# Carrying an expert's rows back to the tokens behind the next expert's second gate and up products

## The chip, the cores and the metric

The kernel runs on one core of a Trainium2 chip (trn2). The metric is the device time of one execution in microseconds (us). The core has a matrix engine (TensorE, called PE in the profile, with its weight loads as PEld), VectorE (DVE), ScalarE (ACT), GpSimd (POOL) and SyncE (SP). In this kernel SP issues the loads of the weights.

## The reference

A model of four layers on 256 tokens of 1024 channels: retention, forgetting attention, then a conformer convolution with a dense feed-forward layer, and a short gated convolution with a mixture of eight experts. The change lies in the mixture of experts, which takes the second half of the time:

```python
logits = (x @ w_router).astype(jnp.float32)
top_val, top_idx = lax.top_k(logits, 2)
wts = jax.nn.softmax(top_val, axis=-1)
gates = jnp.sum(one_hot(top_idx, 8) * wts[..., None], axis=-2)
out = jnp.zeros_like(x)
for e in range(8):
    h = silu(x @ w_gate[e]) * (x @ w_up[e])      # 1024 -> 3584
    out = out + gates[..., e:e + 1] * (h @ w_down[e])   # 3584 -> 1024
```

A layer norm of alpha * x + out follows and is the output. All of it is in float32.

## The kernel before, in words

**Weights.** All weights are streamed from memory once, in units of 1 MB ([128, 2048] in float32). `Stream` (lines 66 to 161) loads them ahead into a ring of raw tiles, ten of them in the expert phase; SP issues a load as soon as a tile is free. Before its use each unit is split exactly into a high part (`wH`, a cast on ScalarE, line 122) and a low part (`wL`, a subtraction on VectorE, line 123). There are three buffers for each part, so a unit can be split only when the unit three before it has been used. Every product is then three matmuls (`mm3`, lines 229 to 233): high by high, high by low, low by high. In the expert phase a unit is split in one piece.

**Experts.** The tokens of each expert are gathered into 128 slots beforehand, transposed and split (`gather_steps`, two experts at a time, in the steps n = 2 to 6 of the experts 1, 3 and 5). For each expert e there are seven steps n, each for 512 of the 3584 hidden columns. The loop of lines 1493 to 1518 writes one step as follows:

- `up(e, n)` (line 1371): the gate product (two units, 24 matmuls of 512 columns), its SiLU on ScalarE into `mh`, the up product (two units, 24 matmuls), and VectorE's multiplication of the two (line 1378).
- `down(*prev)` (line 1390): the down product of the step before (two units, 24 matmuls) into the expert's two accumulator banks `y[e]`. The first unit and the second unit each go through both halves of the output columns.
- `turn(h)` (line 1381): four transposes of the new `h` and the split of the result into `mhH` and `mhL`.

So the last down product of expert e - 1 stands in step 0 of expert e. Behind it, in step 0, come for each half `nh` of the 1024 columns:

- `y_split(e - 1, nh)` (line 1426): a cast on ScalarE and a subtraction on VectorE, from the accumulator bank into the tile of tag `hL` (one buffer). In the trace these are `hL<-acc` of lines 358 and 361.
- `slots_back(e - 1, nh)` (line 1430): per token tile one PSUM bank and two matmuls of 512 columns with the one-hot rows `ohT`, of the high and of the low part (lines 1437 and 1438). This is what carries the slots' rows back to the tokens.
- `add_back(e - 1, nh)` (line 1442): per token tile one VectorE instruction (line 1446) that multiplies by the router's gate and adds to the running sum `self.o`, which the trace calls `x`.

**PSUM.** Two pools of four banks each: `mm` (line 215) for gate and up products, transposes and carry-backs, and `acc` (line 218) for the accumulators `y[e]`, two banks for each expert.

**The order of the work.** The program is written in the order above, and a scheduler puts instructions on each engine's queue by that order as a priority: an instruction that by its model cannot start yet may be passed by a later one that can. Each engine then works through its queue strictly in that order and waits at the first instruction whose inputs or buffer are not there. A bank or buffer is handed to the next user when its last reader is through. `self.soon` (line 211) raises the priority of what is written inside it. The last expert's end (`down_last`, line 1403) has a carry-back of its own, which the change doesn't touch. A second pass over slots 128 to 255 stands behind a branch (line 1558).

Of the kernel before, what the change touches and what calls it, by code (L numbers as in the profile page):

```python
# [65 lines left out]
class Stream:  # L66
    """Weights in the order of their use: 1 MB loads run ahead as far as the rings of raw tiles
    allow, then each is split exactly into two parts that fp32r passes carry."""

    def __init__(self, K, split_bufs, pieces=2):  # L70
        self.K, self.SB, self.pieces = K, split_bufs, pieces
        self.units, self.raws, self.parts = [], {}, {}
        self.rings = []
        self.i = self.nl = self.ns = 0
        self.native = None
        self.side = {}
        self.after = 0      # units whose split stays behind what has been traced so far

    def beside(self, fn):
        """fn issues loads of its own in front of the next unit's."""  # L80
        self.side.setdefault(len(self.units), []).append(fn)

    def ring(self, pool, tag, bufs, upto=1 << 30):
        """Buffers for the raw units before unit upto."""
        self.rings.insert(0, [pool, tag, bufs, 0, upto])
# [50 lines left out]
    def ahead(self, n, behind=True):  # L136
        """Splits the next n units, behind what has been traced so far."""
        self.after = max(0, self.i + n - self.ns) if behind else 0
        self._split(self.i + n)

    def get(self, key, hold=0):
        """The next unit; hold: units got before that are still to be used."""
        k, _, split = self.units[self.i]
        assert k == key, (k, key)
        if self.native is not None:
            self.native[3] -= 1
            self.native = None
        self._split(self.i + 1)
        ahead = 0
        j = self.i + 1  # L150
        while j < len(self.units) and ahead < self.SB - 1 - hold:
            ahead += self.units[j][2]
            j += 1
        self._split(j)
        self._load()
        r = self.parts.pop(self.i)
        self.i += 1
        if not split:
            self.native = r[1]
            return r[0]  # L160
        return r
# [31 lines left out]
class Kern:  # L193
# [9 lines left out]
    def table(self, func, after):  # L203
        """Has ACT load func's table off the critical path, once `after` is there."""
        self.nc.scalar.activation(self.t(self.sp, [P, 1], "tab", bufs=2), after, func)

    def ld(self, dst, src):
        """A load that keeps its place among those of the weights."""
        self.tc.keep_in_program_order(self.nc.sync.dma_start(out=dst, in_=src))

    def soon(self, n=400):
        """What is traced inside goes ahead of work traced up to n instructions before."""
        return self.tc.high_priority(n)
# [21 lines left out]
    def behind(self, ins, prev):  # L235
        """ins goes after prev on their engine."""
        self.tc.add_manual_dep(ins.ins, prev.ins.name,
                               mybir.DependencyInfo(mybir.DependencyClass.NoSync, mybir.DependencyReason.DATA),
                               reason="order")

# [1 line left out]
    def proj_tok(self, key, after=None, begun=False):  # L242
        """[t, 512] per token tile, from two units of four k blocks; begun: by first_tok."""
        if begun:
            ps = self.fps
            self.tok_tile(self.fw, ps, 0, 1)
        else:
            ps = [self.mm() for _ in range(2)]
        for kh in range(begun, 2):
            self.tok_half(key, ps, kh)  # L250
            if after is not None:
                after()
        return ps

    def first_tok(self, key):
        """The first token tile's part of the first unit of a phase."""
        self.fps = [self.mm() for _ in range(2)]
        self.fw = self.st.get(key, 2)
        self.behind(self.tok_tile(self.fw, self.fps, 0, 0), self.pair_end)

    def proj_wst(self, key, hH, hL):
        """[n, t] for two blocks of 128 n, from one unit of eight k blocks."""
# [9 lines left out]
    def first_half(self, key):  # L272
        """The first token tile's part of a phase's first product, which needs nothing of the second tile."""
# [14 lines left out]
    def proj_two(self, key, key2, begun, between):  # L288
        """Two products as of proj_wst; between takes the first, returns the second. begun: by first_half."""
# [20 lines left out]
    def out_k2(self, key, acc, oH, oL, ks, first, last):  # L310
        """acc[tt][nh] += o[k block].T @ w rows, one unit of two k blocks; oH(k, tt) an AP."""
# [8 lines left out]
    def out_k4(self, key, acc, oH, oL, ks, nh, first, last):  # L320
        """The same for one half of n, one unit of four k blocks."""
# [7 lines left out]
    def out_last(self, key, acc, oH, oL, parts):  # L329
        """The last two units of a product, a token tile at a time; parts: (k blocks, nh, first, last) of each."""  # L330
# [32 lines left out]
    def rpow(self, src, n, eps, scale=1.0, tag="rstd"):  # L363
        """(src * scale + eps) ** -0.5 for a [128, n] AP."""
# [7 lines left out]
    def ln_stats(self, parts, eps):  # L372
        """mean and rstd ([128, 1] each) over the free axis of a list of [128, 512] APs."""
# [11 lines left out]
    def new_h(self, f=True, parts=True):  # L385
        """Channels by tokens, [128, 8, 256]: f32 and the two parts of it."""
# [4 lines left out]
    def turned(self, x, tt, nh):  # L391
        """x.T of one token tile and half of the channels: [128, 4, 128] in a bank."""
# [8 lines left out]
    def plain(self, x, tt):  # L401
        """Token tile tt of x into hT or hH and hL."""
# [9 lines left out]
    def affine(self, x, tt, A, B, f, H, L, func=AF.Identity):  # L412
        """func(A*x.T + B) of token tile tt, and its parts; A, B: [128, 8]."""
# [56 lines left out]
    def vectors(self):  # L470
        """The vectors along partitions."""
# [14 lines left out]
    def mod_start(self, parts):  # L486
        """Bias of four chunks of 512 columns, one per 32 partitions, and the sums' bank."""
# [20 lines left out]
    def shift_scale(self, m, i):  # L508
        """m: chunks shift lo, shift hi, scale lo, scale hi -> A = g*(1+scale), B = shift, [128, 8]."""
# [13 lines left out]
    def gate_row(self, m, i):  # L523
        """m: chunks gate0 lo, hi, gate1 lo, hi -> row i spread over the partitions, [128, 1024]."""
# [9 lines left out]
    def residual(self, acc, gate, tt):  # L534
        """x + gate * acc of token tile tt, and rsqrt of its mean square."""
# [216 lines left out]
    def fox(self):  # L752
# [3 lines left out]
        with self.tc.tile_pool(name="fox", bufs=1) as fp:  # L756
# [11 lines left out]
            def decay(ps):  # L768
                """log forget gates, [t, 16] per token tile."""
# [24 lines left out]
            def running(lf):  # L794
                """Their running sums."""
# [14 lines left out]
            def qk(key, g, is_q, begun=False):  # L810
                """Normed heads with the decay's columns: [t, head, 64 | 2] per token tile."""
# [32 lines left out]
            def stage_t(d):  # L844
                """Transposed q and k of one head, with the gains."""
# [35 lines left out]
            def stage_v(d0, d1):  # L881
                """o.T of two heads into oT[:, pair, :]."""
# [87 lines left out]
    def rows(self, g, b):  # L970
        """Vectors along the free axis, spread over the partitions."""
# [5 lines left out]
    def deepnorm(self, acc, gb, first, f=False, parts=True):  # L977
        """x = LN(alpha*x + acc)*g + b and its transposed parts; first() follows those of the first token tile."""
# [26 lines left out]
    def conv_rows(self):  # L1005
        """Tap rows by tap mod 4, the upper half of the channels 32 partitions further on, and the
        first 256 channels' as they are from partition 64 on."""
# [11 lines left out]
    def conv_weights(self):  # L1019
        """Taps as [tap mod 4 and channel, group of 32 channels, tap block], and by channel, [128, 2, 31]."""  # L1020
# [14 lines left out]
    def conformer(self):  # L1035
        nc = self.nc
        hH, hL = self.hH, self.hL
        with self.tc.tile_pool(name="conf", bufs=1) as cp:
# [71 lines left out]
            def taps_apart(k, js):  # L1110
                """A block of channels, tap by tap."""
# [118 lines left out]
    def route(self, tt):  # L1230
        """Router of one token tile: which two experts."""
# [27 lines left out]
    def slots(self, tt):  # L1259
        """The slots of one token tile in the first two experts."""  # L1260
# [15 lines left out]
    def counts(self):  # L1276
        """Tokens of each expert."""
# [15 lines left out]
    def route_weights(self, pool):  # L1293
        """Softmax over the two chosen logits, zero elsewhere; the largest count as an integer."""
# [23 lines left out]
    def gather_steps(self, es, base, oh=None, bank=None):  # L1318
        """Slots base..base+127 of the tokens of two experts: transposed parts per expert, and
        the one-hot rows that carry slots back to tokens; five steps, the last yields them."""  # L1320
# [34 lines left out]
    def experts(self, st, base):  # L1355
        """All experts over their slots base..base+127; adds their gated rows to self.o."""
# [46 lines left out]
        def down_last(e, HL):  # L1403
            """The last rows of the last expert, half of the columns at a time."""
# [25 lines left out]
        def slots_back(e, nh, yHL):  # L1430
            """The slots' rows at their tokens, of half of the columns."""
# [18 lines left out]
        def dense_gates():  # L1450
            """The first gates of the first expert, for all tokens: needs no routing."""
# [12 lines left out]
        def dense_gather(h, HLs):  # L1464
            """The rows of the first expert's slots."""
# [27 lines left out]
        for e, n in [(e, n) for e in range(N_EXP) for n in range(7)]:  # L1493
# [9 lines left out]
            else:  # L1503
                h = up(e, n, None, lambda: None)
            down(*prev)
            with self.soon(60 if st.i >= len(st.units) - 2 else 0):
                prev = (e, n, turn(h))
            if e and n == 0:
                yHL = y_parts()
                for nh in range(2):  # L1510
                    y_split(e - 1, nh, yHL)
                    add_back(e - 1, nh, slots_back(e - 1, nh, yHL))
# [8 lines left out]
    def rest(self):  # L1521
        """Gates, alpha * x and the largest count."""
# [117 lines left out]
    def startup(self):  # L1640
        """The first block's input, half of the channels at a time, and with each half the products that it allows."""
# [143 lines left out]
```

## Time and profile before

| what | us |
|---|---|
| median of 3 runs | 1878.39 |
| lowest and highest run | 1877.34, 1884.4 |
| span of the profiled execution | 1873.6 |
| PE busy | 1809.3 |
| VectorE busy | 1415.0 |
| ScalarE busy | 1064.7 |

The span runs from the first to the last instruction of one profiled execution. No time of that execution from outside is listed, so its span stands beside the median of the runs: 1878.39 - 1873.6 = 4.8 us lie around it. A matmul of 512 columns shows as some 0.4 us long though the next one starts 0.23 us after it, since matmuls are pipelined; so the starts are what counts. Idle time in brackets at the end of a row is the engine's idle time just before the instruction, and what ended it.

### The profile page before, as it was taken

To read this page: it belongs to the slowest core of one execution; us is meant where nothing else is said; L and a number is where in the kernel's file an instruction comes from. 1 tells how busy PE (TensorE), PEld (TensorE's weight loads), DVE (VectorE), ACT (ScalarE), POOL (GpSimd) and SP (SyncE) were. 2 spreads that over 40 slices of the span, in tenths; PEclk is the share of its full clock that TensorE was granted. 3 is DMA by queue.
4 is the path that set the end of the run, shared out by engine and by line. 5 is a ranking of instruction groups with operands and counts; after the bars stand their busy time and mean duration, and the time that the engine had idled before them with its cause. 6 is when DMAs were issued, how large, how long until landed. Compare 5 with 4: busy or idle time off the path is not lost. (4 is left out here: it accounts for less than half of the span.)

```text
span 1873.6 us, 24361 instructions
## 1 busy us (share of the span) xinstructions
PE 1809.3 (97%) x9741; PEld 1486.5 (79%) x9741; DVE 1415.0 (76%) x1469; ACT 1064.7 (57%) x1036; POOL 65.7 (4%) x112
## 2 busy tenths in 40 slices
PE   6999999999999999999999999999999999999996
PEld 3867778789689998987878878878778788788785
DVE  3656666667775557679888888888888888888887
ACT  3333445654443433347767767767767677677673
POOL 1000003001100001000000000000000000000000
PEclk9999999999999999999999999999999999999998
DMA  9677646237356557548999989999999999999991
GB/s 356 233 274 243 224 141 202 77 113 252 114 180 190 188 184 243 195 147 316 346 359 340 362 297 363 369 340 337 349 319 365 360 342 355 316 349 366 332 365 68
DMA packets 252615, 509.34 MB, mean 272 GB/s; under 512 B 12347, under 2 KB 68782, under 8 KB 251470
## 3 DMA queue, kind: packets, MB, share of 16 engines
q1 hardware_dynamic: 249550, 500.64, 76.3%
q0 software_dynamic: 2592, 6.97, 1.2%
q8 instruction: 78, 1.28, 0.3%
q14 instruction: 43, 0.35, 0.1%
q10 hardware_dynamic: 352, 0.10, 0.0%
HBM read 504.28 MB, written 1.05 MB: 270 GB/s over the span
## 5 line engine op out<-in xcount | busy, mean ns | idle before, releaser
L123 DVE TENSOR_TENSOR wL<-raw,wH 128x2048 fp32r<-128x2048 f32 (+2 forms) x582 | 1033.9, 1801 | 258.7 <-ACT wH L122 257.6
L122 ACT CAST wH<-raw 128x2048 fp32r<-128x2048 f32 (+2 forms) x582 | 870.4, 1517 | 466.4 <-PE mm L233 144.3
L231 PE MATMUL mm<-hH,wH 128*128 128x256 f32 x816 | 232.2, 285 | 0.0
L232 PE MATMUL mm<-hL,wH 128*128 128x256 f32 x816 | 231.6, 284 | 0.0
L233 PE MATMUL mm<-hH,wL 128*128 128x256 f32 x816 | 231.2, 283 | 0.3 <-DVE wL L123 0.3
L231 PE MATMUL mm<-wH,hH 128*128 128x512 f32 (+1 forms) x512 | 200.4, 393 | 4.9 <-ACT wH L122 2.6
L232 PE MATMUL mm<-wL,hH 128*128 128x512 f32 (+1 forms) x512 | 199.4, 389 | 1.0 <-DVE wL L123 1.0
L232 PE MATMUL acc<-wL,mhH 128*128 128x512 f32 x448 | 178.5, 399 | 0.0
L233 PE MATMUL acc<-wH,mhL 128*128 128x512 f32 x448 | 176.6, 394 | 0.0
L231 PE MATMUL acc<-wH,mhH 128*128 128x512 f32 x448 | 166.8, 395 | 0.0
L231 PEld LDWEIGHTS mm<-hH,wH 128*128 128x128 f32 x816 | 156.5, 192 | 5.4 <-ACT wH L122 2.5
L233 PEld LDWEIGHTS mm<-hH,wL 128*128 128x128 f32 x816 | 156.5, 192 | 1.4 <-DVE wL L123 1.3
L232 PEld LDWEIGHTS mm<-hL,wH 128*128 128x128 f32 x816 | 156.6, 192 | 0.6 <-issue 0.2
L231 PE MATMUL mm<-wH,hT 128*128 128x512 f32 x336 | 133.1, 396 | 3.5 <-DVE x L1446 3.5
L231 PE MATMUL mm<-wH,xg 128*128 128x512 f32 x328 | 131.0, 399 | 3.5 <-DVE x L1446 3.5
L232 PE MATMUL mm<-wL,hT 128*128 128x512 f32 x336 | 132.7, 395 | 0.4 <-DVE wL L123 0.4
L233 PE MATMUL mm<-wH,hT 128*128 128x512 f32 x336 | 132.0, 393 | 0.0
L232 PE MATMUL mm<-wL,xg 128*128 128x512 f32 x328 | 130.8, 399 | 0.1
L233 PE MATMUL mm<-wH,xg 128*128 128x512 f32 x328 | 130.0, 396 | 0.0
L231 PEld LDWEIGHTS mm<-wH,hH 128*128 128x128 f32 x512 | 98.2, 192 | 30.9 <-ACT wH L122 3.6
L232 PEld LDWEIGHTS mm<-wL,hH 128*128 128x128 f32 x512 | 98.3, 192 | 21.7 <-DVE wL L123 3.5
L233 PE MATMUL mm<-wH,hL 128*128 128x512 f32 (+1 forms) x288 | 110.9, 385 | 0.7 <-DVE hL L361 0.7
(376 smaller groups left out, 2422.6 us busy)
## 6 DMA issues: line engine op xcount, KB each, us to landing
raw<-in_moe_w_gate_dram SPq DMA_DIRECT2D x112, 1024.0 KB
raw<-in_moe_w_up_dram SPq DMA_DIRECT2D x112, 1024.0 KB
raw<-in_moe_w_down_dram SPq DMA_DIRECT2D x111, 1024.0 KB
raw<-in_ret_w_in_dram SPq DMA_DIRECT2D x24, 1024.0 KB
raw<-in_mod_w_dram SPq DMA_DIRECT2D x32, 512.0 KB
raw<-in_fox_w_in_dram SPq DMA_DIRECT2D x16, 1024.0 KB
raw<-in_sc_w_in_dram SPq DMA_DIRECT2D x12, 1024.0 KB
raw<-in_ffn_w_gate_dram SPq DMA_DIRECT2D x11, 1024.0 KB
```

Of the source, the lines that this page charges most:

```text
L122: ops = (K.nc.scalar.copy(H[:, s], raw[:, s]), K.nc.vector.tensor_tensor(L[:, s], raw[:, s], H[:, s], op=ALU.subtract))
L123: K.nc.vector.tensor_tensor(L[:, s], raw[:, s], H[:, s], op=ALU.subtract))
L231: self.mm_first = mmul(ps, sH, mH, start=first, stop=False)
L232: mmul(ps, sH, mL, start=False, stop=False)
L233: self.mm_last = mmul(ps, sL, mH, start=False, stop=last)
```

## The change

The carry-back and the add are taken out of the loop over halves behind the split, in step 0, and stand in step 1 of the same expert, behind its gate and up products and ahead of the down product of step 0. The split stays where it was. The last expert's end stays as it was. The rest of the diff empties comments and docstrings, line by line, so that the lines above this place keep their numbers.

```diff
                 prev = (0, 0, turned[0])
             else:
                 h = up(e, n, None, lambda: None)
+            if e and n == 1:
+                for nh in range(2):
+                    add_back(e - 1, nh, slots_back(e - 1, nh, yHL))
             down(*prev)
             with self.soon(60 if st.i >= len(st.units) - 2 else 0):
                 prev = (e, n, turn(h))
...
                 yHL = y_parts()
                 for nh in range(2):
                     y_split(e - 1, nh, yHL)
-                    add_back(e - 1, nh, slots_back(e - 1, nh, yHL))
             if e % 2 and e < N_EXP - 1 and n >= 2:
```

## Rows read from the trace of the kernel before

**Rows 1.** The page's span and its totals by engine: busy us, share of the span, instructions.

```profile
span 1873.6 us, 24361 instructions
PE 1809.3 (97%) x9741; PEld 1486.5 (79%) x9741; DVE 1415.0 (76%) x1469; ACT 1064.7 (57%) x1036; POOL 65.7 (4%) x112
```

**Rows 2.** Windows: the seven steps with a carry-back, with their sum; columns in Rows 3.

```profile
971.70:992.61 20.91, 19.71 (x85) 15.22 (x84) 18.62 (x15) 13.41 (x10) 0.00 (x0) 1.00 0.91 315
1098.57:1123.29 24.72, 22.34 (x86) 17.24 (x84) 19.29 (x15) 13.30 (x10) 0.00 (x0) 0.86 0.77 268
1225.19:1247.45 22.26, 19.66 (x86) 15.16 (x84) 19.36 (x15) 13.38 (x10) 0.00 (x0) 1.00 0.91 315
1355.62:1379.20 23.58, 20.98 (x85) 16.31 (x84) 19.22 (x15) 13.39 (x10) 0.00 (x0) 0.93 0.84 285
1480.79:1502.81 22.02, 19.42 (x85) 15.17 (x84) 19.22 (x15) 13.39 (x10) 0.00 (x0) 1.00 0.90 323
1609.04:1632.83 23.79, 21.19 (x85) 16.30 (x84) 19.43 (x15) 13.39 (x10) 0.00 (x0) 0.93 0.83 285
1735.96:1759.45 23.49, 20.89 (x86) 16.30 (x85) 19.32 (x15) 13.39 (x10) 0.00 (x0) 0.93 0.86 301
sum 160.77, PE 144.19 PEld 111.70 DVE 134.46 ACT 93.67 POOL 0.00; mean PE 20.60 PEld 15.96 DVE 19.21 ACT 13.38 POOL 0.00
```

**Rows 3.** Windows: the seven plain steps behind those, first and sum, under the columns.

```profile
core 0: us, PE busy (x) PEld busy (x) DVE busy (x) ACT busy (x) POOL busy (x), PEclk, DMA share, GB/s
992.61:1009.57 16.96, 16.96 (x78) 13.88 (x76) 14.87 (x9) 12.43 (x8) 0.00 (x0) 1.00 1.02 372
...
sum 119.27, PE 119.27 PEld 97.13 DVE 100.96 ACT 87.08 POOL 0.00; mean PE 17.04 PEld 13.88 DVE 14.42 ACT 12.44 POOL 0.00
```

**Rows 4.** Waits of PE from 860 to 1830 us: total us, times, longest.

```profile
PE mm L231 <- DVE x L1446: 8.9, 5, 1.8
PE mm L1437 <- ACT hL L358: 5.1, 6, 0.9
```

**Rows 5.** Timeline of PE at the change to expert 5: start us, us, instruction.

```profile
1486.83 0.63 PE L1437 MATMUL mm<-hL,ohT 128*128 128x512 f32 x2
...
1488.78 0.73 PE L1437 MATMUL mm<-hL,ohT 128*128 128x512 f32 x2 [0.83 <-ACT hL L358]
1491.29 0.50 PE L231 MATMUL mm<-wH,hH 128*128 128x512 f32 x1 [1.77 <-DVE x L1446]
```

**Rows 6.** Timeline of DVE, the same change and the two steps behind it.

```profile
1488.28 2.29 DVE L123 TENSOR_TENSOR wL<-raw,wH 128x2048 fp32r<-128x2048 f32 x1 [0.51 <-ACT wH L122]
1490.49 1.40 DVE L1446 SCALAR_TENSOR_TENSOR x<-mm,rgate,x 128x512 f32<-128x512 f32 x2
1491.81 0.68 DVE L361 TENSOR_TENSOR hL<-acc,hL 128x512 fp32r<-128x512 f32 x1
...
1499.99 4.54 DVE L123 TENSOR_TENSOR wL<-raw,wH 128x2048 fp32r<-128x2048 f32 x2 [0.92 <-ACT wH L122]
1504.45 0.68 DVE L1378 TENSOR_TENSOR mh<-mh,mm 128x512 f32<-128x512 f32 x1
...
1519.97 0.69 DVE L1378 TENSOR_TENSOR mh<-mh,mm 128x512 f32<-128x512 f32 x1 [0.73 <-PE mm L233]
```

**Rows 7.** Timeline of ACT at the same change.

```profile
1485.86 0.58 ACT L358 CAST hL<-acc 128x512 fp32r<-128x512 f32 x1 [0.57 <-PE acc L233]
1486.34 1.91 ACT L122 CAST wH<-raw 128x2048 fp32r<-128x2048 f32 x1
```

**Rows 8.** Windows: the start, the expert phase, a stretch without carry-back; columns as Rows 3.

```profile
10.00:50.00 40.00, 32.77 (x214) 19.83 (x207) 19.21 (x36) 14.76 (x23) 4.61 (x9) 0.91 1.05 385
860.00:1820.00 960.00, 942.82 (x4199) 763.10 (x4199) 822.74 (x506) 675.11 (x472) 1.10 (x2) 0.99 0.97 348
...
1379.20:1480.79 101.59, 101.59 (x457) 83.31 (x456) 88.06 (x48) 74.44 (x48) 0.00 (x0) 1.00 1.01 365
```

**Rows 9.** Waits of ACT over the whole span: total us, times, longest.

```profile
ACT wH L122 <- DMA raw<-in_ret_w_in_dram: 70.9, 14, 7.2
```

## The prediction

> **What bounds the kernel now.** I read the totals first, then the run in stretches, then the waits of the matrix engine, then one expert change in order of time, and last the transfers.
>
> The span is 1873.6 us and the matrix engine (PE) is busy for 97% of it [rows 1]. That share alone says little, so I cut the expert phase into steps: one step runs from the first matmul of a down product to the first of the next. In a plain step PE is busy for the whole step at the full granted clock: 16.96 us of 16.96 [rows 3]. The phase is bound by PE, except where experts change. There are seven changes, and their steps last 20.91 to 24.72 us, with PE busy short of the step and, in four of them, a granted clock of 0.86 to 0.93 [rows 2]. Those are the steps in which rows are carried back.
>
> How much is lost there? The seven steps sum to 160.77 us [rows 2]; the seven plain steps right behind them, of the same experts, sum to 119.27 us [rows 3]. A change step has eight more matmuls (two halves of the columns, two token tiles, two parts). A plain step holds 72 matmuls of 512 columns and four transposes of 128, as long as 73 together, so one takes 119.27 / (7 x 73) = 0.233 us. 56 x 0.233 = 13.05 us is work, and 160.77 - 119.27 - 13.05 = **28.45 us is lost**, 4.06 us for each change.
>
> Where? The waits of PE in the phase have two large entries: a gate product that waits for an add (8.9 us, five times) and a carry-back matmul that waits for a cast of the expert's sum (5.1 us, six times) [rows 4]. The change to expert 5 shows both. The carry-back starts at 1486.83, the third of its four banks waits 0.83 us for the second half's cast, and then the next gate product waits 1.77 us, until 1491.29, for a PSUM bank [rows 5]. The pool has four; turned rows and carry-backs hold them, and VectorE frees one only with its add at 1490.49, behind a weight subtraction of 2.29 us [rows 6]. The rest of the loss is the lowered clock behind some of these idle times (1.2 GHz instead of 2.4 GHz for a part of the step) and what precedes the waits.
>
> **The change, part by part.** It moves 8 matmuls on PE and 4 adds on VectorE per change of expert, seven times. It adds and removes none, issues no DMA, and moves nothing past SP's or POOL's queue. The split of the sums (two casts, two subtractions) stays where it is.
>
> *Old place, waits removed.* PE goes from the down product straight to the next gate product, which needs one bank and finds it, because no carry-back holds any. Both waits above go, and the clock drop behind them. At most 28.45 us.
>
> *Old place, what is late next.* The split of the sums still stands in ScalarE's queue: at expert 5 the first cast idles 0.57 us for the down product to end its first half, and only then, at 1486.34, comes the cast of the second gate unit [rows 7]. Its subtraction starts at 1488.28 and ends at 1490.57 [rows 6]. Today PE is waiting anyway. Without the wait, PE starts the gate product at 1486.83, is through its first unit of 12 matmuls at 1486.83 + 12 x 0.233 = 1489.63, and needs the subtraction from the next unit's second matmul on, at 1489.86: 0.7 us of waiting. Then the second half's own subtraction (0.68 us) goes ahead of the next unit's (2.29 us), which ends at 1493.54, while PE wants it at 1490.57 + 12 x 0.233 = 1493.37: 0.2 us more. I take the same for six changes; the change to expert 1 loses least today (20.91 us [rows 2]) and I give it none. 6 x 0.9 = 5.4 us. Bounds: nothing, if the casts come in another order, and 7 x 1.77 = 12.4 us (the bank wait of today) if the splits fall further behind.
>
> *New place, PE.* Behind the second step's up product three of four banks are free: the turned rows' is long released, the gate's is released by its activation, one is unused. The first three carry-back pairs can run, 6 x 0.233 = 1.4 us. The fourth needs the up product's bank, which VectorE frees by multiplying gate and up. In the plain step that multiplication starts 0.73 us after VectorE fell idle, straight behind the product; at expert 5's second step it stands behind two subtractions and starts at 1504.45, 1.64 us after the product's end at 1502.81 (the second window edge) and ends at 1505.13 [rows 2, 6]. In the first case PE hardly waits. In the second it waits 1505.13 - 1502.81 - 1.4 = 0.9 us. Half-way is 0.45 us, 7 x 0.45 = 3.2 us. Bounds: nothing (the down product's matmuls, which need no bank of this pool, can fill the gap) and 1.77 us each, the bank wait that PE shows today: 12.4 us.
>
> *New place, VectorE.* Four adds of 0.70 us [rows 6], 2.8 us, now stand ahead of the subtraction for the third step's first gate unit. From the late multiplication: adds until 1507.9, subtraction until 1510.2. PE gets there after 8 carry-backs and 24 down matmuls: 1502.81 + 32 x 0.233 = 1510.3. So it is just covered, by the down product; I cost it at nothing. If that cover were gone, PE would wait up to 2.8 us.
>
> *Held longer.* The split sums' buffer is wanted again six steps later, the one-hot rows have three buffers, and the accumulator banks are freed by the split, which doesn't move. No cost.
>
> *Transfers.* A faster phase asks for more: 348 GB/s on average over 960 us [rows 8] becomes 348 x 960 / (960 - 20) = 355 GB/s. The plain stretch of expert 4 already runs at 365 GB/s for 102 us, and the start, where ScalarE waits 70.9 us for loads [rows 9], moves 385 GB/s [rows 8]. No cost.
>
> **Sum:** 28.45 - 5.4 - 3.2 = 19.85 us gained. The profiled span of 1873.6 us becomes 1853.7 us. The median of the runs, 1878.39 us, is 4.8 us above the span, and I take what lies around it as unchanged: **1858.5 us**.
>
> **Rivals.** *The stall only moves.* Carry-back and adds still meet VectorE's queue and four banks. If each change keeps what the mildest of the usual patterns loses today (expert 5: 22.02 - 16.96 - 1.87 = 3.2 us [rows 2, 3]), 22.4 us stay, the gain is 6 us: 1872.4 us, which counts as the same. For it speaks that the new place's multiplication is late after a change; against it that a whole down product that needs no such bank follows. 0.09.
>
> *Loads become the bound.* The ten raw buffers could be drained in plain steps and filled in today's stalls; then the rate over the phase would be the ceiling and nearly nothing is gained: about 1876 us. The 385 GB/s at the start and the absence of any large wait for a load in this phase speak against it. 0.05.
>
> The Trainium skill, "DMA: Bandwidth & Descriptors", section Bandwidth, measured 341 GB/s for a transfer of 1 MB issued from GpSimd, the size that each load has here. Taken as a ceiling for these loads it would leave no gain at all. The trace disagrees: 348 GB/s over the phase and 365 GB/s in a plain stretch.
>
> *Slower.* One mechanism: the fourth carry-back stands in PE's order ahead of the down product, and its bank hangs on a multiplication that VectorE does only behind two subtractions more. PE then idles 0.9 + 2 x 2.29 = 5.5 us, and the clock drop comes on top, 1.5 us (23.49 against 22.02 us, two changes with like waits [rows 2]). 7.0 us at seven changes is 49 us against 28.45 us removed: 1899 us. It makes the kernel slower from 4.06 us a change on. Against it: a bank wait that long does not occur anywhere in the phase, the longest is 1.8 us [rows 4]. 0.05.
>
> That the matmuls are not moved at all, since the program's order is a priority and not a command, would show as the old waits; I count it with the first rival.
>
> **How the numbers follow.** The forecast gets 0.81, the stall that moves 0.09, the loads 0.05, the slower case 0.05. About 0.5% (9.4 us) is what a measurement of this kernel can tell from no change, so the forecast counts as faster, the next two as the same. Low end: all of the loss is recovered, 1878.4 - 28.5 = 1849.9, say 1850. High end: late subtractions at all seven changes (7 x 0.9 = 6.3 us) and the upper bound of 12.4 us at the new place leave 9.75 us: 1868.6, say 1869. The other upper bound, with 3.2 us at the new place, ends at 1865.5. Both bounds at once I leave out, since a PE that waits lets VectorE catch up.
>
> **What would show it.** Change steps of 19 to 21 us with a granted clock of 1.00; no wait of PE for an add; PE waits of under 1 us for weight subtractions in the first gate product; second steps longer than plain ones by 1.9 to 2.8 us. Wrong it would be if a bank wait of over 2 us stands at the new place, or if loads hold up the casts.

## The result, and the profile after

| what | before | after |
|---|---|---|
| median of 4 runs, us | 1878.29 | 1854.95 |
| lowest and highest run, us | 1877.34, 1884.4 | 1853.81, 1857.9 |
| span of the profiled execution, us | 1873.6 | 1856.1 |
| first down product to the last, 54 steps, us | 976.05 | 954.67 |

The ratio of the runs is 0.9871, 95% interval 0.9851 to 0.9891: faster by 23.3 us, where 19.85 us were forecast (1858.5 us, range 1850 to 1869). The two spans differ by 17.5 us only. The profiled execution after is the slowest of its four runs, and its first down product starts at 872.60 us, 4.0 us later than before (868.58 us). That is a matter of the part before the experts, which the change does not touch. So the experiments below are read by the 54 steps from the first matmul of the first down product to the first of the last; there 21.4 us went, and two profiled executions of the changed kernel gave 954.67 us both times.

The windows of the changed kernel, cut as [rows 2], show the seven steps in which experts change; columns as in [rows 3].

```profile
975.72:994.07 18.35, 18.35 (x83) 15.02 (x82) 17.21 (x11) 14.62 (x11) 0.00 (x0) 1.00 1.00 358
1101.32:1121.20 19.88, 19.17 (x86) 15.33 (x85) 17.41 (x13) 14.28 (x11) 0.00 (x0) 1.00 0.98 342
1223.14:1243.12 19.98, 19.37 (x86) 15.31 (x85) 17.45 (x13) 14.27 (x11) 0.00 (x0) 1.00 1.00 363
1351.37:1371.19 19.82, 19.15 (x86) 15.32 (x84) 17.41 (x13) 14.27 (x11) 0.00 (x0) 1.00 0.98 346
1472.85:1492.68 19.83, 19.13 (x86) 15.32 (x85) 17.41 (x13) 14.27 (x11) 0.00 (x0) 1.00 0.97 349
1599.04:1619.02 19.98, 19.37 (x85) 15.31 (x84) 17.44 (x13) 14.27 (x11) 0.00 (x0) 1.00 0.95 342
1722.17:1742.00 19.83, 19.12 (x85) 15.32 (x84) 17.41 (x13) 14.27 (x11) 0.00 (x0) 1.00 1.01 370
sum 137.67, PE 133.65 PEld 106.94 DVE 121.73 ACT 100.23 POOL 0.00; mean PE 19.09 PEld 15.28 DVE 17.39 ACT 14.32 POOL 0.00
```

The sum fell from 160.77 to 137.67 us, and the granted clock is 1.00 in all seven, where four had less. The steps right behind, which were plain in [rows 3], take a little of it back, 120.18 instead of 119.27 us; half of that is a carry-back pair of the change to expert 1, which runs in the step behind it (the first row here):

```profile
994.07:1011.50 17.43, 17.43 (x79) 14.25 (x78) 15.94 (x13) 11.24 (x8) 0.00 (x0) 1.00 0.94 335
...
sum 120.18, PE 120.18 PEld 97.51 DVE 110.09 ACT 80.09 POOL 0.00; mean PE 17.17 PEld 13.93 DVE 15.73 ACT 11.44 POOL 0.00
```

Together 23.10 - 0.91 = 22.19 us. Of the loss of 28.45 us, 6.26 us are left. The waits of PE in the expert phase (total us, times, longest) say which: both entries of [rows 4] are gone, and the wait for a weight's subtraction has grown.

```profile
PE mm L232 <- DVE wL L123: 4.9, 8, 0.7
PE mm L1469 <- ACT mhH L358: 1.3, 1, 1.3
PE mm L1384 <- DVE mh L1378: 0.2, 1, 0.2
```

Six of the eight waits in the first row, 0.61 to 0.71 us each and 4.0 us together, stand at the changes to experts 2 to 7, one at each. The other two, 0.42 us each, lie in other steps, and what the other two rows show lies outside the changes too.

The change to expert 5 in order of time, from the timeline of PE (compare [rows 5]):

```profile
1478.65 0.39 PE L233 MATMUL acc<-wH,mhL 128*128 128x512 f32 x1
1478.87 0.39 PE L231 MATMUL mm<-wH,hH 128*128 128x512 f32 x1
...
1482.68 0.50 PE L232 MATMUL mm<-wL,hH 128*128 128x512 f32 x1 [0.70 <-DVE wL L123]
...
1485.55 0.39 PE L1437 MATMUL mm<-hL,ohT 128*128 128x512 f32 x1
...
1488.51 0.39 PE L1438 MATMUL mm<-hL,ohT 128*128 128x512 f32 x1
1488.74 0.40 PE L1437 MATMUL mm<-hL,ohT 128*128 128x512 f32 x1
...
1492.44 0.39 PE L1438 MATMUL mm<-hL,ohT 128*128 128x512 f32 x1
1492.68 0.40 PE L231 MATMUL acc<-wH,mhH 128*128 128x512 f32 x1
```

The gate product follows the down product without a gap. Its second unit waits 0.70 us for a subtraction. The carry-back does not stand in one block behind the up product: the first matmul sits inside the up product at 1485.55, others at 1488.51 and 1488.74, and the rest close it. None waits. The timeline of VectorE beside it (compare [rows 6]), with the late subtraction at 1480.34, and the adds spread among the weights:

```profile
1480.34 2.29 DVE L123 TENSOR_TENSOR wL<-raw,wH 128x2048 fp32r<-128x2048 f32 x1 [0.52 <-ACT wH L122]
1482.55 0.68 DVE L361 TENSOR_TENSOR hL<-acc,hL 128x512 fp32r<-128x512 f32 x1
...
1488.94 0.75 DVE L1446 SCALAR_TENSOR_TENSOR x<-mm,rgate,x 128x512 f32<-128x512 f32 x1 [1.31 <-PE mm L1438]
...
1491.81 0.68 DVE L1378 TENSOR_TENSOR mh<-mh,mm 128x512 f32<-128x512 f32 x1
1492.40 0.75 DVE L1446 SCALAR_TENSOR_TENSOR x<-mm,rgate,x 128x512 f32<-128x512 f32 x1
```

The change to expert 1 looks different. Three carry-back pairs follow the up product, from 992.67 us on. The multiplication, which frees the up product's bank, stands behind two subtractions and starts only at 994.30; the fourth pair comes at 995.24. PE does not wait: five matmuls of the down product go ahead of that pair. From the timelines of PE and VectorE:

```profile
992.67 0.39 PE L1437 MATMUL mm<-hL,ohT 128*128 128x512 f32 x1
...
994.07 0.39 PE L231 MATMUL acc<-wH,mhH 128*128 128x512 f32 x1
...
995.24 0.40 PE L1437 MATMUL mm<-hL,ohT 128*128 128x512 f32 x1
```

```profile
989.85 4.53 DVE L123 TENSOR_TENSOR wL<-raw,wH 128x2048 fp32r<-128x2048 f32 x2 [0.70 <-ACT wH L122]
994.30 0.68 DVE L1378 TENSOR_TENSOR mh<-mh,mm 128x512 f32<-128x512 f32 x1
```

### The profile page after: what moved, and what is told of

The parts are those of the page before. It is cut to its first block, busy times and chain, and to the rows that moved or that the text cites. A ratio compares the mean times of both kernels' runs of the same rounds, so it can differ in the third digit from the quotient of the medians.

```text
span 1856.1 us, 24359 instructions
## 1 busy us (share of the span) xinstructions
PE 1804.0 (97%) x9741; PEld 1485.4 (80%) x9741; DVE 1412.2 (76%) x1469; ACT 1063.9 (57%) x1036; POOL 65.7 (4%) x112
```

## The experiments

All ratios are to the kernel before, which ran in turn on the same chip. The third column is the length of the 54 steps in the profile, the fourth PE's waits at the seven changes of expert. Waits for weights' subtractions in other steps, 0.4 to 0.9 us in each run, are not in it.

| run | ratio, 95% interval | 54 steps, us | waits of PE at the changes, us |
|---|---|---|---|
| before | 1 | 976.05 | add 9.1, cast 5.1, other subtractions 2.4 |
| changed kernel | 0.9871, 0.9851 to 0.9891 | 954.67 | weights' subtraction 4.0 |
| e1_acc_banks | 0.9876, 0.9854 to 0.9897 | 952.73 | weights' subtraction 0.9 |
| e2_split_between | 0.9893, 0.9875 to 0.9912 | 954.61 | weights' subtraction 4.0 |
| e3_carry_between | 0.9868, 0.9849 to 0.9886 | 951.63 | add 0.9, weights' cast 0.6 |
| e4_no_carry | 0.9831, 0.9811 to 0.9851 | 941.15 | weights' subtraction 3.9 |
| e5_halves_apart | 0.9988, 0.9973 to 1.0004 | 979.20 | split's subtraction 11.5, cast 4.6 |
| e6_split_behind_cast | 0.9846, 0.9811 to 0.9881 | 948.48 | none |
| e7_carry_pinned | 0.9867, 0.9834 to 0.9901 | 954.23 | weights' subtraction 4.0 |
| e8_between_and_cast | 0.9862, 0.9829 to 0.9895 | 952.92 | add 2.2, weights' cast 0.6 |
| e9_old_place_cast | 0.9948, 0.9930 to 0.9965 | 968.21 | split's subtraction 7.4, cast 3.9, add 0.5 |
| e10_after_again | 0.9879, 0.9858 to 0.9901 | 954.67 | weights' subtraction 4.0 |
| e11_split_behind_again | 0.9845, 0.9823 to 0.9868 | 948.52 | none |

**Other banks at the old place.**

```diff
-                    add_back(e - 1, nh, slots_back(e - 1, nh, yHL))
+                    add_back(e - 1, nh, slots_back(e - 1, nh, yHL, self.acc))
```

(the last argument is the pool that the carry-back takes its banks from; this is the kernel before otherwise)

> The carry-back stays at its old place, but its banks come from the accumulators' pool, where two are free in step 0, so that the gate product of the next step has a bank at once. Theory (two waits and the lowered clock behind them): the gate product's wait for an add (8.9 us) goes, and most of the clock drop with it (half of some 9.6 us); waits for casts or subtractions of 0.7 us a change stay. 1878 - 9 - 5 = 1864 us, between 1858 and 1868. Rival one (banks alone): nearly all of the gain of the change, 1853 to 1857 us. Rival two (it is the carry-back's place behind the split that counts, whatever the bank): 1873 us or more.

The phase took 952.73 us, the ratio is 0.9876: the whole gain without moving anything. Rival one held. My theory had put a part of the old loss on the wait for the cast, as if it stood by itself. The timeline of PE at the change to expert 5 in this run:

```profile
1473.27 0.40 PE L1437 MATMUL acc<-hL,ohT 128*128 128x512 f32 x1
1473.50 0.40 PE L231 MATMUL mm<-wH,hH 128*128 128x512 f32 x1
...
1474.43 0.63 PE L1438 MATMUL acc<-hL,ohT 128*128 128x512 f32 x2
1474.89 0.39 PE L232 MATMUL mm<-wL,hH 128*128 128x512 f32 x1
1475.12 0.40 PE L1437 MATMUL acc<-hL,ohT 128*128 128x512 f32 x1
```

Once the gate product has a bank, it starts between the carry-backs, and these are queued where their inputs are there. So free banks are enough to remove both old waits. Without one, the gate product stood in PE's queue behind the carry-backs, and PE had nothing to do while the split ran. The order of the casts has a share of its own in these waits, as the last run below shows.

**The halves split first, at the old place.**

```diff
                     y_split(e - 1, nh, yHL)
+                for nh in range(2):
                     add_back(e - 1, nh, slots_back(e - 1, nh, yHL))
```

> The kernel before, with both halves split first and then both carried back, at the old place and with the old banks. Theory (a bank of the products' pool is what the old place lacks; the gate product stands behind four carry-backs that hold all four): nothing changes for it, the gate product still waits 1 to 2 us a change for an add, 1873 to 1879 us. Rival (the old wait comes from the order of the halves, the second cast behind the first half's carry-back): 1865 us or less.

No difference by the interval, so the order of the halves was not the cause. But the wait is not the one that I expected: no add stands at the head of PE's waits (total us, times, longest), the carry-backs themselves wait for the split.

```profile
PE mm L1438 <- DVE hL L361: 11.5, 7, 2.0
PE mm L1437 <- ACT hL L358: 4.6, 6, 0.8
```

With the same four banks the idle time at the old place stays, and the name of what ended it changes with the order in the queue.

**The carry-back with 24 matmuls of cover.** Cover means matmuls that PE can run while the split is under way. The change's three lines go into the gap between the gate and the up product of step 1:

```diff
-                h = up(e, n, None, lambda: None)
-            if e and n == 1:
-                for nh in range(2):
-                    add_back(e - 1, nh, slots_back(e - 1, nh, yHL))
+                h = up(e, n, None, lambda: [add_back(e - 1, nh, slots_back(e - 1, nh, yHL)) for nh in range(2)])
```

(for n == 1; otherwise as before)

> The changed kernel, with the carry-back written between the gate and the up product of step 1, so with 24 matmuls of cover and not 48, and with an up product behind it that needs a bank of the same pool. Theory: one product (5.6 us) covers the split, but the up product has to wait for a bank until an add is through: 0 to 1.8 us a change, 1855 to 1867 us, likeliest 1859. Rival (the cover alone counts, a bank is always found): 1855 us within 1.

951.63 us, 3.0 us less than the changed kernel in the phase, and not to be told from it by the ratio. The theory's wait of the up product did not come; the rival is the nearer one, though the run is faster than both say (0.9868 of 1878.29 us is 1853.5 us). The up product finds its bank; only 0.9 us of waits for adds came in, at the carry-backs themselves. A part of the carry-back now fills the time in which the weights' subtraction is late. It does not have the cover of its place in the program: at the change to expert 5 it begins right behind the first matmul of the gate product.

```profile
1477.09 0.40 PE L231 MATMUL mm<-wH,hH 128*128 128x512 f32 x1
1477.32 0.63 PE L1437 MATMUL mm<-hL,ohT 128*128 128x512 f32 x2
```

So this run has the old banks, and its carry-back begins nearly at the old place and is spread over the products. The gate product has its bank first. That fits the bank as the cause, though the carry-back's place in the queue differs from the old one too.

**The carry-back held behind the up product.** Every carry-back pair is ordered behind the last matmul of the up product of step 1, in the changed kernel:

```diff
-                nc.tensor.matmul(ps, ot, yHL[:, 0, s], start=True, stop=False)
+                o = nc.tensor.matmul(ps, ot, yHL[:, 0, s], start=True, stop=False)
+                if after is not None:
+                    self.behind(o, after)
```

(`after` is `self.mm_last`, the last matmul traced before, which is the up product's)

> The changed kernel, with the eight carry-back matmuls held on TensorE behind the last matmul of the up product, where the program writes them, and not let into the products before. Theory (the prediction's: three banks are free, the fourth carry-back pair waits for the multiplication): 0 to 0.9 us of bank waits a change, 0 to 6 us slower than the changed kernel, likeliest 3. Rival one (the gaps of the products are what makes the carry-back cheap): 8 us slower or more. Rival two (no bank wait at all, the place alone counts): the same within 1 us in the expert phase.

Rival two: 954.23 us, and no wait for a bank. PE's second to fourth pair and VectorE's multiplication at the change to expert 5, from the two timelines of this run:

```profile
1485.84 0.39 PE L1437 MATMUL mm<-hL,ohT 128*128 128x512 f32 x1
...
1486.30 0.39 PE L1437 MATMUL mm<-hL,ohT 128*128 128x512 f32 x1
...
1486.77 0.39 PE L1437 MATMUL mm<-hL,ohT 128*128 128x512 f32 x1
```

```profile
1485.57 0.69 DVE L1378 TENSOR_TENSOR mh<-mh,mm 128x512 f32<-128x512 f32 x1 [0.79 <-PE mm L233]
```

The multiplication starts right behind the product, ends at 1486.26, and the fourth pair needs the bank at 1486.77. At the change to expert 1 it is late as in the changed kernel, and the fourth pair again stands behind five matmuls of the down product.

**No carry-back.** The carry-backs and adds of experts 0 to 6 are left out, so their part of the sum is missing from the output.

> The changed kernel without the carry-back and the adds of experts 0 to 6 (the splits stay), so that part of the sum is left out. Theory: in the changed kernel the carry-back costs nothing but its own matmuls on TensorE, 56 x 0.233 = 13.05 us, and the adds are hidden: 1855 - 13 = 1842 us, between 1840 and 1844. Rival (the 28 adds of 0.70 us on VectorE, 19.6 us, still cost something through late subtractions): below 1840 us.

The phase is 954.67 - 941.15 = 13.5 us shorter, against 13.05 us of matmuls: the adds are hidden, and so is everything else of the carry-back, to within 0.5 us. The runs say less: 1839.86 to 1846.59 us, with a ratio of 0.9831 whose distance to the changed kernel's is only 7.5 us, and each ratio has an interval of some 4 us on either side.

**The split moved.** In the changed kernel, `y_split` is written between the gate and the up product of step 1.

> The changed kernel, with the split of the sums moved as well, to between the gate and the up product of step 1. Theory (what is left at the old place is the weight subtraction that the split makes late, 0.7 us at six changes): these 4 us go, 1855 - 4 = 1851 us, with no wait of PE over 0.5 us at a change. Rival (the split makes another subtraction late wherever it stands, since VectorE's queue is the same): 1855 us, with waits of 0.5 us or more inside the up product or the down product.

The phase is the same, 954.61 us, with the same waits. The queues explain it: the scheduler put the casts and subtractions on ScalarE and VectorE where they stood before, save for one cast and seven subtractions that changed places with a neighbour or two. The edit did not do what it says, so it decides nothing about the cause.

**The split held.** The same question with an order that the scheduler has to keep:

```diff
         def y_split(e, nh, yHL, after=None):
...
+            o = nc.scalar.copy(yHL[:, 0, s], y[e][nh])
+            if after is not None:
+                self.behind(o, after)
...
-                    y_split(e - 1, nh, yHL)
+                    y_split(e - 1, nh, yHL, st.last[0])
```

(`st.last[0]` is the cast of the gate product's second unit, the last one traced)

> The changed kernel, with the split's casts held on ScalarE behind the cast of the next product's second gate unit. Theory (the late weight subtraction, 0.6 to 0.7 us at six changes, comes from ScalarE standing at the split's cast): these waits go, the expert phase of the profile shrinks by 4 us, 1851 us on the scale on which the changed kernel has 1855. Rival (VectorE has no room there, whatever ScalarE does): the waits stay at 0.5 us or more, no change.

948.48 us, 6.2 us less. ScalarE does the weight's cast first, then both halves' casts in one go; PE's waits at the changes shrink from 4.0 us to none; the two that the last row below shows stand in other steps, as they do in the changed kernel. From this run's timeline of ScalarE at the change to expert 5, and its waits of PE:

```profile
1469.49 1.91 ACT L122 CAST wH<-raw 128x2048 fp32r<-128x2048 f32 x1
1471.30 1.07 ACT L1428 CAST hL<-acc 128x512 fp32r<-128x512 f32 x2
```

```profile
PE mm L232 <- DVE wL L123: 0.9, 2, 0.4
```

The seven change steps and the seven behind them, cut as before, have these sums:

```profile
sum 131.90, PE 131.90 PEld 107.39 DVE 123.37 ACT 97.08 POOL 0.00; mean PE 18.84 PEld 15.34 DVE 17.62 ACT 13.87 POOL 0.00
...
sum 119.72, PE 119.72 PEld 97.24 DVE 108.95 ACT 82.97 POOL 0.00; mean PE 17.10 PEld 13.89 DVE 15.56 ACT 11.85 POOL 0.00
```

Together they take 251.62 us. Twice the plain steps and the carry-back's matmuls make 2 x 119.27 + 13.05 = 251.59 us. So of the old loss of 28.45 us nothing is left, and not only the waits went but also the slower matmuls around them.

Run again beside the changed kernel on one chip:

> The changed kernel again, beside the next run on the same chip. Every theory: a ratio of 0.987 to the kernel before, 954 to 955 us for the 54 steps of the profile's expert phase.

> The sixth run's kernel again, to compare with the changed kernel on the same chip. Theory: 4 to 6 us faster than it in the runs' medians, 948 to 949 us for the expert phase. Rival (its better time came from the part of the program before the experts): the same as the changed kernel within 2 us.

1849.84 us (1847.39 to 1851.5) against 1856.86 us (1852.9 to 1858.66): 7.0 us, ranges that do not meet, and 948.52 against 954.67 us in the phase. This is the version that beats both kernels. Of the 7.0 us, the phase shows 6.2 us; in the profiled executions the experts also start earlier in the second (868.04 against 872.75 us), in a part that the edit does not touch.

**Both small leftovers.** The place of the carry-back as in e3_carry_between, with the held casts of e6_split_behind_cast:

> The carry-back written between the gate and the up product of step 1, and the split's casts held as in the other run of this call. Theory (both small leftovers gone, the late subtraction and nothing new): the expert phase 4 to 5 us shorter than in the changed kernel, 1850 us on its scale. Rival (without the early carry-backs behind the down product as a filler the subtraction is late again): no shorter than the changed kernel.

952.92 us: 1.8 us less than the changed kernel and more than either edit alone. The held split comes later, and the carry-backs wait longer for adds (2.2 us against 0.9 us). Neither expectation was met.

**The held casts at the old place.**

> The kernel before, with the split's casts held on ScalarE behind the cast of the next product's second gate unit, as in the sixth run, and the carry-back at its old place with its old banks. Theory (without free banks at the old place no order of the casts helps; the gate product still stands behind carry-backs that need the split and behind adds): no faster than before, 1874 to 1886 us, with waits of TensorE of 15 us or more at the seven changes. Rival (the late cast is the common cause of the old loss): 1868 us or less.

The theory was wrong: the ratio is 0.9948, the phase 968.21 us, 7.8 us less than before, over a third of what the change brings. The rival came near its number (0.9948 of 1878.29 us is 1868.5 us), but the late cast is the cause of a part of the old loss only. Carry-backs still wait at all changes, but less, and the clock is below 1.00 in two changes instead of four; in these windows one without and one with:

```profile
1097.94:1118.96 21.02, 19.77 (x85) 15.19 (x84) 19.12 (x15) 13.43 (x10) 0.00 (x0) 1.00 0.94 328
...
1728.22:1751.04 22.82, 20.94 (x86) 16.20 (x85) 19.23 (x15) 13.32 (x10) 0.00 (x0) 0.93 0.89 309
```

So the order of the casts has its own share at the old place too. With the gate product behind the carry-backs it does not remove the wait.

## Why the prediction was right, point by point

**What bounds.** Right: PE, except at seven changes, with 28.45 us lost there. The run without carry-back puts its bare cost at 13.5 us, where 13.05 us were taken as work.

**Waits removed at the old place.** Right in size. The idle time of PE in the 54 steps fell by 17.0 - 4.87 = 12.1 us (lengths less busy times: 976.05 - 959.05 = 17.0 us before, 954.67 - 949.80 = 4.87 us after), and the rest, some 9 us, is busy time of PE. The four change steps that had a lowered clock lost 8.6 us of busy time, the other three 1.9 us, and the steps behind them took 0.9 us back (the rows above against [rows 2]). The cause was stated too loosely: the two waits were told as two. The run with other banks shows that free banks remove both.

**Late subtraction, 5.4 us.** Right in mechanism, nearly in size: 0.7 us were expected at six changes and none at expert 1; PE waited 0.61 to 0.71 us at exactly those six, 4.0 us together. The second term of 0.2 us did not come. The held casts show the cause, since they take the wait away. They took 6.2 us with it, so the late subtraction cost more than its waits: some 2.2 us were slower matmuls around them, for which the prediction had no term.

**Bank wait at the new place, 3.2 us.** This term failed: no run with the carry-back at the new place has a wait of PE for a bank. It read the time of the multiplication from a step behind an old stall (1504.45 in [rows 6]), where VectorE was catching up on two subtractions. With the stall gone, the multiplication is on time at six changes, so the bank is free, even when the carry-backs are held together. At the change to expert 1 it is as late as was feared (994.30 - 992.67 = 1.63 us), and it still costs nothing, because matmuls of the down product fill the gap. That was the lower bound which the prediction gave for this term. That the carry-backs would be let into the products was not foreseen and turned out not to matter: 954.23 against 954.67 us.

**The sum.** 19.85 us were forecast; the runs gave 23.3 us, the phase 21.4 us, the pairs of steps 22.2 us. Of the lost 28.45 us, 8.6 us were expected to stay and 6.26 us did: 6.2 us for the late subtraction instead of 5.4 us, and nothing for the bank instead of 3.2 us. So the failed term was partly made up by one that was too small, and the nearness of the sum is in part luck.

**Span and median.** The 4.8 us between them do not all lie around the span. Every timed run lists its time and its span, and these differ by 1.7 to 1.9 us (1857.9 against 1856.1 us, for one). So the profiled execution before must have been some 3 us faster than the median. The forecast was taken from the median by a difference, so it is not touched.

**VectorE's adds, cost nothing.** Right: 13.5 us for a carry-back whose matmuls take 13.05 us.

**Transfers.** Right: the phase ran at 351 GB/s after, 353 GB/s with the held split and 356 GB/s without carry-back, and each of these shows a single wait for a load there, of 0.8 us on ScalarE. The 341 GB/s for a 1 MB transfer in the Trainium skill, "DMA: Bandwidth & Descriptors", section Bandwidth, was no ceiling for these loads.

**The rivals.** The stall did not move, and the loads did not bind. The slower case needed PE to idle 5.5 us at the fourth pair; the one change where that pair hangs on a late multiplication, to expert 1, shows no wait.

**The signs.** No wait for an add, waits under 1 us for weights' subtractions and a clock of 1.00 came as said. The change steps took 19.82 to 19.98 us, within 19 to 21 us, except the one to expert 1 with 18.35 us, whose last pair runs a step later. Second steps longer by 1.9 to 2.8 us did not show: the windows behind the changes are longer by 0.91 / 7 = 0.13 us each. The moved matmuls stand ahead of the down product at which a window is cut, so they count in the change steps.

## What to carry to other kernels

When an engine waits in one place for several things, ask what else it could have run there: here the next product lacked a PSUM bank, so TensorE stood in a queue of small matmuls until their inputs came. More banks at that place, or an order in which the next product takes its bank before the small matmuls, took back 21 to 24 us in the 54 steps; with the casts held as well, nothing of the 28.45 us was left in the changed kernel. And do not price a new place only by a row that stands in the wake of the stall which the change removes: take a row from an undisturbed step too, and look what else the engine has to run if the row is late all the same.

## What the runs showed of the hardware that was not expected

**Equal waits, unequal price.** In the kernel before, the changes to experts 3 to 7 show the same waits of 0.83 and 1.77 us, but the granted clock fell in those to 4, 6 and 7 and not in those to 3 and 5; against the plain step behind each, the first three lost 4.7 us, the other two 3.2 us, each beside 1.87 us of work. So the same idle time cost 1.5 us more where the clock fell behind it.

**The part before the experts.** The first down product starts at 867.4 to 868.6 us in some profiles and at 872.0 to 873.2 us in others, whatever the kernel. One place where they differ is the stretch behind a 3.06 us wait of PE in the convolution, first for the changed kernel, then for the last run:

```profile
505.00:525.00 20.00, 16.93 (x117) 13.09 (x108) 11.47 (x22) 9.85 (x22) 0.72 (x1) 0.83 0.00 1
```

```profile
505.00:525.00 20.00, 15.97 (x98) 12.09 (x91) 12.97 (x24) 11.86 (x24) 0.72 (x1) 1.00 0.10 34
```

All six profiles with a clock of 1.00 here started the experts early. Of seven with 0.83 or 0.91, five started them late and two early (the kernel before, at 868.58 us, is one). The same seven show a second fall of the clock between 831 and 844 us, the six do not. What else adds to it was not tried.

**Two paces.** Plain steps (without carry-back or gathering, and not right behind a change) of experts 0, 3 and 6 take 17.22 to 17.25 us, those of the others 16.91 to 16.97 us, in every run. These three keep their gathered rows in a tile of their own (`xg`), the others in tiles that they share with earlier layers. Whether the tile is the reason was not tried.
